# Index scores of two heads on the two halves of the array's rows, and one bank for the probabilities' transposes

## Chip, cores and metric

One core of a Trainium2 chip. The metric is the time of one execution on the device in microseconds; the lower the better. The time before is the median of three runs.

## What is computed

A two-layer decoder step over a prompt of 2048 tokens and a small sample group. The change lies in layer 0, in the sparse attention of the prompt. For each query a lightning indexer scores all earlier keys, the best 256 are kept, and attention runs over those:

```python
N_HEADS, N_KV_HEADS, HEAD_DIM, N_IDX_HEADS, IDX_DIM, TOPK_MAX, SEQ = 8, 2, 128, 16, 64, 256, 2048

def indexer_select(qi, wi, ki, q_pos, k_sel):
    dots = jnp.einsum('thd,ld->thl', qi.astype(F32), ki.astype(F32))
    score = jnp.einsum('th,thl->tl', wi.astype(F32), jax.nn.relu(dots))
    admissible = jnp.arange(ki.shape[0])[None, :] <= q_pos[:, None]
    score = jnp.where(admissible, score, -jnp.inf)
    _, idx = lax.top_k(score, k_sel)
    valid = idx <= q_pos[:, None]
    return idx, valid
```

The dots contract over 64 values only, half of the array's 128 rows. The results are held to the precision of float32, so the kernel splits each float32 operand into a part that the fast format float32r holds exactly (hi) and the rest (lo), and adds up the products of the parts.

## The kernel before

The program has three phases. Phase A projects all tokens (tiles of 128 tokens, groups of 360 to 512 output columns, each product as three matmuls hi x hi, lo x hi and hi x lo by `mm3`, L327). Phase B is the attention over query tiles, in groups of two tiles in the order of `B_ORDER` (L135). Phase C is the recurrent layer. Tiles are allocated from pools with a fixed number of buffers, and a scheduler of the framework sets the order of the instructions on each engine from their dependences, priorities and buffers; each engine then works in that order.

**Index scores** (`indexer`, L1197). Units are pieces of up to 512 keys of a query tile (`widths`, L1126). For the first group, tiles 14 and 15, `index` (L1101) in `phase_a` weaves them into the end of the projection; for the others `phase_b` (L1483) merges them with the attention of the group before. `index_queries` (L1177) loads four heads of a query block (`qiload`), splits hi and lo on POOL into the two halves of 128 columns (`qis`), transposes each head on PE (`qips`), and ACT copies the four to `qiT`: rows 0 to 63 hold the head's hi, rows 64 to 127 its lo. The keys stand in `ki_hi` and `ki_lo`, each twice, in rows 0 to 63 and again in rows 64 to 127 (`prep_index`, L1149). So two matmuls over all 128 rows (L1218, L1219) give one head's dots with all four products of parts, in a PSUM tile `dots` of one bank. ACT applies relu (L1222), and the weighted sum over heads goes on on POOL for the first `gp` heads (3 by `GP_HEADS`, L138; L1225 to L1228) and on DVE for the others (L1230). POOL's heads of a unit are issued a unit ahead, between DVE's heads of the unit before.

**Attention** (`attend_unit` L1404, `attend_scores` L1424, `attend_values` L1446). For each head PE computes the scores `s` in pieces of up to 512 keys, DVE adds the mask and takes the maximum, ACT takes the exponential (`sp`, L1442). For the head before, PE transposes the probabilities in fours into `pt_ps` (L1465), ACT copies them to `pt` (L1467), and PE multiplies with the values into `o_ps` (L1455; one fp32 matmul of the program is two in the trace). The queries' transposes `qps` (L1416) and two small ones use the same PSUM tag.

**PSUM.** There are eight banks. In phase B two are for `s`, three for `dots` (which `qips`, `kps` of `prep_keys` and, at the end, the tiles of `first_chunk` use too), two for `pt_ps` and `qps`, one for `o_ps`. While the index is woven into phase A, four banks are for `dots`.

Of the kernel before, what the change touches and what calls it, by code (L numbers as in the profile page):

```python
# [11 lines left out]
F32 = mybir.dt.float32  # L12
F32R = mybir.dt.float32r
# [4 lines left out]
ALU = mybir.AluOpType  # L18
# [119 lines left out]
GP_HEADS = (3, 3, 3, 3, 3, 3, 3)  # L138
# [848 lines left out]
def phase_a(k):  # L987
    nc, tc = k.nc, k.tc
    with ExitStack() as es:
# [111 lines left out]
        def index():  # L1101
# [3 lines left out]
            with (  # L1105
                tc.tile_pool(name="a_ps3", reuse_waits="tile", bufs=4, space=PSUM) as pd,
# [70 lines left out]
def index_queries(k, qt, hh, pool, pd, tag):  # L1177

    nc = k.nc
    qi = pool.tile([P, 4, ID], F32, tag="qiload", name="qiload", bufs=1)  # L1180
    nc.sync.dma_start(qi, k.qi_d[qt][:, hh * 256 : hh * 256 + 256].rearrange("p (h d) -> p h d", d=ID))
    qs = pool.tile([P, 4, 2 * ID], F32R, tag="qis", name="qis", bufs=1)
    nc.gpsimd.tensor_scalar(qs[:, :, :ID], qi, 1.0, 0.0, ALU.mult, ALU.add)
    nc.gpsimd.tensor_tensor(qs[:, :, ID:], qi, qs[:, :, :ID].bitcast(F32), ALU.subtract)
    t = pool.tile([P, 4, P], F32R, tag="qiT", name="qiT", bufs=5)
    ps = pd.tile([P, 4, P], F32, tag=tag, name="qips", bufs=PS_BUFS.get(tag))
    for j in range(4):
        nc.tensor.transpose(ps[:, j, :].bitcast(F32R), qs[:, j, :], k.ident_r)
    nc.scalar.copy(t, ps)
    return t  # L1190
# [6 lines left out]
def indexer(k, tiles, gp, scores, pool, gpool, spool, stag, pd, dtag, ttag, pq=None):  # L1197
# [12 lines left out]
    def head(u, h):  # L1210
        qt, c, w = units[u]
        if qt not in sc:
            sc[qt] = spool.tile([P, S], F32, tag=stag, name="score", bufs=2)
            scores.append(sc[qt])
        acc = sc[qt][:, c : c + w]
        q = qT[qt, h // 4][:, h % 4, :]
        ps = pd.tile([P, 512], F32, tag=dtag, name="dots", bufs=PS_BUFS.get(dtag))
        nc.tensor.matmul(ps[:, :w], q, k.ki_hi[:, c : c + w], start=True, stop=False)  # L1218
        nc.tensor.matmul(ps[:, :w], q, k.ki_lo[:, c : c + w], start=False, stop=True)  # L1219
        eng, rp, tag, bufs = (nc.gpsimd, gpool, *(("relu", 3) if gpool is pool else ("relu_g", 2))) if h < gp else (nc.vector, pool, "relu", 3)  # L1220
        r = rp.tile([P, 512], F32, tag=tag, name="relu", bufs=bufs)
        nc.scalar.activation(r[:, :w], ps[:, :w], AF.Relu, bias=0.0, scale=1.0)  # L1222
        sg = k.sg_all[:, qt, h : h + 1]
        if h == 0:
            eng.tensor_scalar(acc, r[:, :w], sg, 0.0, ALU.mult, ALU.add)  # L1225
        elif h < gp:
            eng.tensor_scalar(r[:, :w], r[:, :w], sg, 0.0, ALU.mult, ALU.add)
            eng.tensor_tensor(acc, acc, r[:, :w], ALU.add)  # L1228
        else:
            eng.scalar_tensor_tensor(acc, r[:, :w], sg, acc, ALU.mult, ALU.add)  # L1230

    load(5 - len(qT))
    for h in range(gp):
        head(0, h)
    every = (IH - gp) // max(gp, 1)
    for u, (qt, c, w) in enumerate(units):
        for n, h in enumerate(range(gp, IH)):
            head(u, h)
            if gp and n % every == 0 and n // every < gp and u + 1 < len(units):
                head(u + 1, n // every)  # L1240
            if h % 4 == 3:
                if c + w == (qt + 1) * P:
                    del qT[qt, h // 4]
                    load(1)
                yield w
        if c + w == (qt + 1) * P:
# [236 lines left out]
def phase_b(k):  # L1483
    nc, tc = k.nc, k.tc
    with ExitStack() as es:
# [5 lines left out]
        pd = es.enter_context(tc.tile_pool(name="b_pd", reuse_waits="tile", bufs=3, space=PSUM))  # L1491
        pps = es.enter_context(tc.tile_pool(name="b_pt", reuse_waits="tile", bufs=2, space=PSUM))
# [630 lines left out]
```

## Time and profile before

| | us |
|---|---|
| median of three runs (3116.81 to 3122.61) | 3120.4 |
| the profiled execution | 3123.55 |
| its span, first to last instruction | 3121.8 |

| engine | busy us | share |
|---|---|---|
| PE (matmuls) | 2892.9 | 93% |
| PEld (weight loads) | 2398.5 | 77% |
| DVE | 2119.0 | 68% |
| ACT | 1656.3 | 53% |
| POOL | 1239.1 | 40% |

Matmuls are pipelined: the duration of one is its latency, several overlap, and what one takes of PE is the distance from its start to the start of the next. A load of weights belongs to each matmul and has a record of its own under PEld. The index scores run from 1037 to 1965 us, the attention from about 1235 to 2170 us.

### The profile page before, as it was taken

Reading aid. Unit: us, or ns where it says so; the run is one execution under the profiler, and the core shown is the slowest. Engines: PE = TensorE matmul, PEld = TensorE weight load, DVE = VectorE, ACT = ScalarE, POOL = GpSimd, SP = SyncE. Lnnn points to the kernel's source line nnn. Section 1 sums busy time; section 2 is a strip of 40 time slices with the busy share of each in tenths; the row PEclk is TensorE's granted clock in tenths of the full one; section 3 lists DMA queues with packets and bytes.
Section 4 is the critical chain, followed back from the end, with each engine's and each line's share of the span. In section 5 each row is a group of like instructions: output and inputs, shape, how many; then the busy total and the mean of one; then the engine's idle time right before and its main releaser. Section 6 shows DMA issues by size and latency. Waiting matters only on the chain. (4 is left out here: it accounts for less than half of the span.)

```text
span 3121.8 us, 46940 instructions
## 1 busy us (share of the span) xinstructions
PE 2892.9 (93%) x16289; PEld 2398.5 (77%) x16289; DVE 2119.0 (68%) x4600; ACT 1656.3 (53%) x3087; POOL 1239.1 (40%) x1277
## 2 busy tenths in 40 slices
PE   6999998889899998899999999998989989999998
PEld 2999885677567887688878888888767777777766
DVE  6755578944444876886788788634786486485486
ACT  5533322543333566777877776644664454464463
POOL 2634445405552442422332332024434544544643
PEclk8999998998989999899999999999999999999989
DMA  7654421245554212200100111133224524423422
GB/s 243 193 155 153 149 73 46 67 136 153 174 164 136 72 58 92 68 16 27 38 30 27 34 37 36 60 122 131 86 68 149 157 71 136 159 85 110 147 75 91
DMA packets 202014, 314.13 MB, mean 101 GB/s; under 512 B 25651, under 2 KB 119487, under 8 KB 201758
## 3 DMA queue, kind: packets, MB, share of 16 engines
q1 hardware_dynamic: 151482, 213.72, 21.5%
q0 software_dynamic: 15792, 51.92, 5.4%
q10 hardware_dynamic: 34484, 45.34, 4.5%
q8 instruction: 129, 2.11, 0.3%
q14 instruction: 127, 1.04, 0.1%
HBM read 254.56 MB, written 56.34 MB: 100 GB/s over the span
## 5 line engine op out<-in xcount | busy, mean ns | idle before, releaser
L1651 POOL TENSOR_TENSOR wlo<-wraw,whi 128x512 fp32r<-128x512 f32 x288 | 415.2, 1457 | 503.4 <-ACT whi L1650 433.9
L1230 DVE SCALAR_TENSOR_TENSOR score<-relu,sg_all,score 128x512 f32<-128x512 f32 (+2 forms) x494 | 363.1, 737 | 82.4 <-ACT relu L1222 64.5
L331 PE MATMUL zps<-whi,hhi 128*128 128x512 f32 (+2 forms) x1024 | 394.9, 387 | 19.7 <-ACT z_q L365 12.0
L333 PE MATMUL zps<-whi,hlo 128*128 128x512 f32 (+2 forms) x1024 | 391.5, 383 | 4.7 <-issue 4.6
L332 PE MATMUL zps<-wlo,hhi 128*128 128x512 f32 (+2 forms) x1024 | 392.7, 384 | 3.3 <-issue 3.2
L1222 ACT ACTIVATE relu<-dots 128x512 f32<-128x512 f32 (+2 forms) x608 | 314.4, 550 | 135.6 <-PE dots L1219 73.8
L1455 PE MATMUL o_ps<-v,pt 128*128 128x128 f32 x2176 | 300.7, 278 | 7.3 <-ACT pt L1467 6.7
L1455 PEld LDWEIGHTS o_ps<-v,pt 128*128 128x128 f32 x2176 | 284.2, 193 | 25.4 <-ACT pt L1467 11.5
L1650 ACT CAST whi<-wraw 128x512 fp32r<-128x512 f32 x288 | 175.5, 617 | 189.8 <-PE ops L333 92.3
L1218 PE MATMUL dots<-ki_hi,qiT 128*128 128x512 f32 (+2 forms) x608 | 249.7, 413 | 14.3 <-ACT relu L1222 10.6
L331 PEld LDWEIGHTS zps<-whi,hhi 128*128 128x128 f32 x1024 | 197.5, 193 | 61.9 <-ACT z_q L365 14.1
L1219 PE MATMUL dots<-ki_lo,qiT 128*128 128x512 f32 (+2 forms) x608 | 227.0, 375 | 0.0
L333 PEld LDWEIGHTS zps<-whi,hlo 128*128 128x128 f32 x1024 | 197.5, 193 | 35.1 <-issue 7.8
L332 PEld LDWEIGHTS zps<-wlo,hhi 128*128 128x128 f32 x1024 | 197.9, 193 | 33.6 <-issue 6.3
L1467 ACT COPY pt<-pt_ps 128x512 f32<-128x512 f32 (+3 forms) x320 | 163.5, 526 | 84.6 <-PE pt_ps L1465 79.4
L332 PE MATMUL zps<-hlo,whi 128*128 128x512 f32 x512 | 201.9, 394 | 0.0
L331 PE MATMUL zps<-hhi,whi 128*128 128x512 f32 x512 | 198.6, 395 | 3.2 <-ACT hhi L180 2.0
L333 PE MATMUL zps<-hhi,wlo 128*128 128x512 f32 x512 | 200.1, 393 | 0.0
L189 POOL TENSOR_TENSOR rs<-ms,mhalf 128x1 f32<-128x1 f32 (+4 forms) x85 | 80.0, 943 | 279.3 <-DVE ms L188 267.1
L1442 ACT ACTIVATE sp<-sp,neg 128x128 f32<-128x128 f32 (+15 forms) x128 | 154.3, 1206 | 65.9 <-POOL neg L1441 64.1
L1465 PE MATMUL pt_ps<-const,sp 128*128 128x128 f32 x1088 | 173.8, 275 | 3.5 <-ACT sp L1442 2.9
L555 ACT COPY s_kT<-s_tp 128x512 f32<-128x512 f32 x128 | 75.1, 586 | 166.6 <-PE s_dots L564 135.5
(582 smaller groups left out, 7325.7 us busy)
## 6 DMA issues: line engine op xcount, KB each, us to landing
wraw<-in_lru_w_in SPq DMA_DIRECT2D x128, 256.0 KB
wraw<-in_attn_w_out SPq DMA_DIRECT2D x64, 256.0 KB
wraw<-in_lru_w_out SPq DMA_DIRECT2D x64, 256.0 KB
wraw<-in_attn_w_in SPq DMA_DIRECT2D x28, 512.0 KB
wraw<-in_attn_w_in ACTq DMA_DIRECT2D x20, 512.0 KB
ada_raw<-in_ada_w SPq DMA_DIRECT2D x16, 512.0 KB
qi_d<-z_qi SPq DMA_DIRECT2D x32, 256.0 KB
q_d<-z_q SPq DMA_DIRECT2D x32, 256.0 KB
```

Source lines behind the costliest of these rows:

```text
L331: mm(ps, ah, bh, start=start, stop=False)
L332: mm(ps, ah, bl, start=False, stop=False)
L333: mm(ps, al, bh, start=False, stop=stop)
L1218: nc.tensor.matmul(ps[:, :w], q, k.ki_hi[:, c : c + w], start=True, stop=False)
L1219: nc.tensor.matmul(ps[:, :w], q, k.ki_lo[:, c : c + w], start=False, stop=True)
L1222: nc.scalar.activation(r[:, :w], ps[:, :w], AF.Relu, bias=0.0, scale=1.0)
L1230: eng.scalar_tensor_tensor(acc, r[:, :w], sg, acc, ALU.mult, ALU.add)
L1455: nc.tensor.matmul(u.o[:, j, :], pt[:, i, :], k.v_sb[k0 + i][:, u.kv * HD : (u.kv + 1) * HD], start=(k0 + i == 0), stop=(k0 + i == u.qt),)
L1465: nc.tensor.transpose(pt_ps[:, i, :], sp[:, (k0 + i) * P : (k0 + i + 1) * P], k.ident)
L1467: nc.scalar.copy(pt[:, :n, :], pt_ps[:, :n, :])
L1650: nc.scalar.copy(hi, raw)
L1651: nc.gpsimd.tensor_tensor(lo, raw, hi.bitcast(F32), ALU.subtract)
```

## The change

Two heads are computed together. `index_queries` no longer splits before the transpose: it transposes two heads at once (one in the first 64 columns, the other in the last 64), and splits afterwards, ACT copying the hi part and DVE subtracting for the lo part. In `qiT` rows 0 to 63 now belong to the even head and rows 64 to 127 to the odd one, and hi and lo are different columns. `pair` issues three products for each head (hi x hi, hi x lo of the keys, lo x hi; the product of the two lo parts is left out), each over 64 rows, the two heads in turns, into a PSUM tile of two banks, one for each head. The program gives these matmuls the array's rows 0 to 63 and 64 to 127. Relu is one instruction over both heads for DVE's heads (and for POOL's in phase A). POOL takes 4 heads instead of 3. In phase B `dots` becomes two tiles of two banks, and `pt_ps` and `qps` share one bank instead of two; `first_chunk` takes one tile of two banks for its four products.

```diff
-GP_HEADS = (3, 3, 3, 3, 3, 3, 3)
+GP_HEADS = (4, 4, 4, 4, 4, 4, 4)
...
-                tc.tile_pool(name="a_ps3", reuse_waits="tile", bufs=4, space=PSUM) as pd,
+                tc.tile_pool(name="a_ps3", reuse_waits="tile", bufs=2, space=PSUM) as pd,
...
-    qi = pool.tile([P, 4, ID], F32, tag="qiload", name="qiload", bufs=1)
-    nc.sync.dma_start(qi, k.qi_d[qt][:, hh * 256 : hh * 256 + 256].rearrange("p (h d) -> p h d", d=ID))
-    qs = pool.tile([P, 4, 2 * ID], F32R, tag="qis", name="qis", bufs=1)
-    nc.gpsimd.tensor_scalar(qs[:, :, :ID], qi, 1.0, 0.0, ALU.mult, ALU.add)
-    nc.gpsimd.tensor_tensor(qs[:, :, ID:], qi, qs[:, :, :ID].bitcast(F32), ALU.subtract)
-    t = pool.tile([P, 4, P], F32R, tag="qiT", name="qiT", bufs=5)
-    ps = pd.tile([P, 4, P], F32, tag=tag, name="qips", bufs=PS_BUFS.get(tag))
-    for j in range(4):
-        nc.tensor.transpose(ps[:, j, :].bitcast(F32R), qs[:, j, :], k.ident_r)
-    nc.scalar.copy(t, ps)
+    qi = pool.tile([P, 2, 2 * ID], F32, tag="qiload", name="qiload", bufs=2)
+    nc.sync.dma_start(qi, k.qi_d[qt][:, hh * 256 : hh * 256 + 256].rearrange("p (h d) -> p h d", d=2 * ID))
+    t = pool.tile([P, 2, 2, P], F32R, tag="qiT", name="qiT", bufs=5)
+    ps = pd.tile([P, 2, P], F32, tag=tag, name="qips", bufs=PS_BUFS.get(tag))
+    for j in range(2):
+        nc.tensor.transpose(ps[:, j, :], qi[:, j, :], k.ident)
+    split_ps(k, t[:, 0], t[:, 1], ps)
     return t
...
-        q = qT[qt, h // 4][:, h % 4, :]
-        ps = pd.tile([P, 512], F32, tag=dtag, name="dots", bufs=PS_BUFS.get(dtag))
-        nc.tensor.matmul(ps[:, :w], q, k.ki_hi[:, c : c + w], start=True, stop=False)
-        nc.tensor.matmul(ps[:, :w], q, k.ki_lo[:, c : c + w], start=False, stop=True)
...
+        q = qT[qt, h // 4]
+        j = h % 4 // 2
+
+        ps = pd.tile([P, 2, 512], F32, tag=dtag, name="dots", bufs=PS_BUFS.get(dtag))
+        kc = slice(c, c + w)
+        for a, b, n in ((0, k.ki_hi, 0), (0, k.ki_lo, 1), (1, k.ki_hi, 2)):
+            for r in range(2):
+                rows = slice(r * ID, r * ID + ID)
+                nc.tensor.matmul(ps[:, r, :w], q[rows, a, j, :], b[rows, kc], start=(n == 0), stop=(n == 2))
+        eng = nc.gpsimd if h < gp else nc.vector
+        if h < gp and gpool is not pool:
+            rr = [gpool.tile([P, 512], F32, tag="relu_g", name="relu", bufs=2)[:, :w] for _ in range(2)]
+            for n in range(2):
+                nc.scalar.activation(rr[n], ps[:, n, :w], AF.Relu, bias=0.0, scale=1.0)
         else:
-            eng.scalar_tensor_tensor(acc, r[:, :w], sg, acc, ALU.mult, ALU.add)
+            both = pool.tile([P, 2, 512], F32, tag="relu", name="relu", bufs=2)
+            nc.scalar.activation(both[:, :, :w], ps[:, :, :w], AF.Relu, bias=0.0, scale=1.0)
+            rr = [both[:, n, :w] for n in range(2)]
...
-        pd = es.enter_context(tc.tile_pool(name="b_pd", reuse_waits="tile", bufs=3, space=PSUM))
-        pps = es.enter_context(tc.tile_pool(name="b_pt", reuse_waits="tile", bufs=2, space=PSUM))
+        pd = es.enter_context(tc.tile_pool(name="b_pd", reuse_waits="tile", bufs=2, space=PSUM))
+        pps = es.enter_context(tc.tile_pool(name="b_pt", reuse_waits="tile", bufs=1, space=PSUM))
...
-            ps = [pps.tile([P, 2, 256], F32, tag=tag, name="ops") for _ in range(2)]
+            ps4 = pps.tile([P, 4, 256], F32, tag=tag, name="ops")
+            ps = [ps4[:, 0:2], ps4[:, 2:4]]
```

The scheduler makes another order of the same work. On PE, in the attention, before (dots are the index scores, s the attention's, pt_ps the transposes of the probabilities):

```order
L1465 MATMUL pt_ps<-const,sp 128x128 x4
L1218 MATMUL dots<-ki_hi,qiT 128x256
L1219 MATMUL dots<-ki_lo,qiT 128x256
L331 MATMUL s<-kT_hi,qTh 128x384
L332 MATMUL s<-kT_lo,qTh 128x384
L333 MATMUL s<-kT_hi,qTl 128x384
L1218 MATMUL dots<-ki_hi,qiT 128x256
L1219 MATMUL dots<-ki_lo,qiT 128x256
```

and after, in the same stage (an "x2" of dots is the couple on the two halves of the rows):

```order
L1222 MATMUL dots<-ki_hi,qiT 128x256 x2
L1222 MATMUL dots<-ki_lo,qiT 128x256 x2
L1222 MATMUL dots<-ki_hi,qiT 128x256 x2
L331 MATMUL s<-kT_hi,qTh 128x512
L332 MATMUL s<-kT_lo,qTh 128x512
L331 MATMUL s<-kT_hi,qTh 128x384
L332 MATMUL s<-kT_lo,qTh 128x384
L1222 MATMUL dots<-ki_hi,qiT 128x512 x2
L1222 MATMUL dots<-ki_lo,qiT 128x512 x2
L1222 MATMUL dots<-ki_hi,qiT 128x512 x2
L1483 MATMUL pt_ps<-const,sp 128x128 x4
```

Single heads, as two matmuls, have become pairs of six matmuls, which still stand between matmuls over the whole array.

The transposes of the probabilities, on PE, before, with the tiles' numbers; the two tiles are two banks:

```order
L333 MATMUL s_18863<-kT_hi_13726,qTl_18623 128x512
L1465 MATMUL pt_ps_18839<-const_60,sp_18736 128x128 x4
L1465 MATMUL pt_ps_18852<-const_60,sp_18736 128x128 x4
L1218 MATMUL dots_18195<-ki_hi_10814,qiT_17530 128x512
L1219 MATMUL dots_18195<-ki_lo_10815,qiT_17530 128x512
```

and after; the two tiles are the same bank, one after the other:

```order
L1473 MATMUL o_ps_23759<-v8_13610,pt_23792 128x128
L1483 MATMUL pt_ps_23839<-const_60,sp_23758 128x128 x4
L1483 MATMUL pt_ps_23852<-const_60,sp_23758 128x128 x4
L1473 MATMUL o_ps_23759<-v0_13602,pt_23844 128x128
L1473 MATMUL o_ps_23759<-v1_13603,pt_23844 128x128
```

The second four stand right behind the first in both, and in the new order the copy by ACT of the first four lies between them.

## Rows read from the trace of the kernel before

**Rows 1.** The page: span, and busy us (share) xinstructions of each engine.
```profile
span 3121.8 us, 46940 instructions
PE 2892.9 (93%) x16289; PEld 2398.5 (77%) x16289; DVE 2119.0 (68%) x4600; ACT 1656.3 (53%) x3087; POOL 1239.1 (40%) x1277
```

**Rows 2.** Table of stretches: length, busy us (instructions) by engine, PE's clock, DMA share, GB/s.
```profile
1030.00:1130.00 100.00, 100.00 (x472) 83.24 (x472) 85.81 (x161) 59.09 (x108) 54.05 (x54) 1.00 0.22 71
...
1340.00:2130.00 790.00, 756.25 (x5309) 686.85 (x5309) 584.48 (x1778) 550.97 (x1070) 221.27 (x326) 0.99 0.14 45
```

**Rows 3.** List by shape, 1030 to 2180 us: busy us, mean ns, idle before, releasers.
```profile
L1218 PE MATMUL dots<-ki_hi,qiT 128*128 128x512 f32 x400 | 175.8, 440 | 11.6 <-ACT relu L1222 8.0 <-DVE tk_up L1294 2.2 <-DVE tk_dn L1295 0.9
...
L1218 PE MATMUL dots<-ki_hi,qiT 128*128 128x384 f32 x112 | 44.3, 396 | 2.4 <-ACT relu L1222 2.4
...
L1218 PE MATMUL dots<-ki_hi,qiT 128*128 128x256 f32 x96 | 30.0, 322 | 0.2 <-ACT relu L1222 0.2
```

**Rows 4.** Timeline of PE at three places: start us, us, line, operation.
```profile
1187.36 0.39 PE L1219 MATMUL dots<-ki_lo,qiT 128*128 128x512 f32 x1
1187.59 0.39 PE L1218 MATMUL dots<-ki_hi,qiT 128*128 128x512 f32 x1
...
96.17 0.34 PE L332 MATMUL zps<-wlo,hhi 128*128 128x384 f32 x1
96.34 0.34 PE L333 MATMUL zps<-whi,hlo 128*128 128x384 f32 x1
...
1504.24 0.29 PE L1218 MATMUL dots<-ki_hi,qiT 128*128 128x256 f32 x1
1504.37 0.28 PE L1219 MATMUL dots<-ki_lo,qiT 128*128 128x256 f32 x1
```

**Rows 5.** Timeline of PE: 32 matmuls in turns on four quarters of the columns.
```profile
784.21 1.08 PE L933 MATMUL sa_o<-sa_v,sa_pT 128*32 128x128 f32 x32
```

**Rows 6.** Timeline of PE: six fp32 matmuls in a line, in the attention.
```profile
1763.73 0.83 PE L1455 MATMUL o_ps<-v,pt 128*128 128x128 f32 x6
```

**Rows 7.** Timeline of PE at 503 us: two matmuls of 4 rows among full ones.
```profile
503.24 0.40 PE L331 MATMUL zps<-whi,hhi 128*128 128x512 f32 x1
503.47 0.39 PE L332 MATMUL zps<-wlo,hhi 128*128 128x512 f32 x1
503.79 0.48 PE L723 MATMUL ss_nps<-ss_mnew,ones 4*128 4x128 f32 x2
504.20 0.50 PE L333 MATMUL zps<-whi,hlo 128*128 128x512 f32 x1
504.54 0.40 PE L331 MATMUL zps<-whi,hhi 128*128 128x512 f32 x1
```

**Rows 8.** Timeline of the weight loads (PEld) at the same place.
```profile
503.24 0.19 PEld L332 LDWEIGHTS zps<-wlo,hhi 128*128 128x128 f32 x1
503.79 0.29 PEld L723 LDWEIGHTS ss_nps<-ss_mnew,ones 4*128 4x128 f32 x2 [0.36 <-issue]
504.20 0.19 PEld L333 LDWEIGHTS zps<-whi,hlo 128*128 128x128 f32 x1
```

**Rows 9.** Timeline of PE: three transposes right behind matmuls on quarters of the columns.
```profile
785.65 0.55 PE L886 MATMUL sa_ktp<-const,sa_k 128*128 128x128 f32 x3
```

**Rows 10.** Timeline of PE: the query transposes of one block of four heads.
```profile
1505.31 0.46 PE L1188 MATMUL qips<-ident_r,qis 128*128 128x128 f32 x4
```

**Rows 11.** List by shape, as rows 3: ACT's copy of four transposes.
```profile
L1467 ACT COPY pt<-pt_ps 128x512 f32<-128x512 f32 x224 | 129.0, 590 | 63.7 <-PE pt_ps L1465 62.1 <-PE o_ps L1455 0.7
```

**Rows 12.** Waits, 1285 to 2130 us: who waited for whom, us, times, longest us.
```profile
PEld dots L1218 <- ACT relu L1222: 16.1, 21, 2.8
...
PE pt_ps L1465 <- ACT pt L1467: 0.5, 2, 0.3
```

**Rows 13.** List by shape, as rows 3: ACT's relu.
```profile
L1222 ACT ACTIVATE relu<-dots 128x512 f32<-128x512 f32 x400 | 229.5, 603 | 100.1 <-PE dots L1219 56.5 <-DVE score L1230 24.8 <-DMA v<-out_v_prompt 3.8
...
L1222 ACT ACTIVATE relu<-dots 128x256 f32<-128x256 f32 x96 | 35.1, 390 | 10.6 <-PE dots L1219 4.7 <-DVE score L1230 1.4 <-PE pt_ps L1465 1.2
```

More of the change, by code (lines that the diff above doesn't have):

```diff
@@ L1208, in load, with pair @@
         del k.index_todo[:n]
-    def head(u, h):
+    def pair(u, h):
         qt, c, w = units[u]
@@ L1215, in head @@
         acc = sc[qt][:, c : c + w]
-        q = qT[qt, h // 4][:, h % 4, :]
-        ps = pd.tile([P, 512], F32, tag=dtag, name="dots", bufs=PS_BUFS.get(dtag))
-        nc.tensor.matmul(ps[:, :w], q, k.ki_hi[:, c : c + w], start=True, stop=False)
-        nc.tensor.matmul(ps[:, :w], q, k.ki_lo[:, c : c + w], start=False, stop=True)
-        eng, rp, tag, bufs = (nc.gpsimd, gpool, *(("relu", 3) if gpool is pool else ("relu_g", 2))) if h < gp else (nc.vector, pool, "relu", 3)
-        r = rp.tile([P, 512], F32, tag=tag, name="relu", bufs=bufs)
@@ L1222, in head @@
[L1222 to L1228, printed above, removed]
-        else:
-            eng.scalar_tensor_tensor(acc, r[:, :w], sg, acc, ALU.mult, ALU.add)
+        q = qT[qt, h // 4]
@@ new lines, in pair, with done @@
+        for n in range(2):
+            sg = k.sg_all[:, qt, h + n : h + n + 1]
+            r = rr[n]
+            if h + n == 0:
+                eng.tensor_scalar(acc, r, sg, 0.0, ALU.mult, ALU.add)
+            elif h < gp:
+                eng.tensor_scalar(r, r, sg, 0.0, ALU.mult, ALU.add)
+                eng.tensor_tensor(acc, acc, r, ALU.add)
+            else:
+                eng.scalar_tensor_tensor(acc, r, sg, acc, ALU.mult, ALU.add)
+    def done(qt, hh):
+        del qT[qt, hh]
+        load(1)
@@ L1232, in indexer @@
     load(5 - len(qT))
-    for h in range(gp):
-        head(0, h)
-    every = (IH - gp) // max(gp, 1)
+    for h in range(0, gp, 2):
+        pair(0, h)
+    pairs = range(gp, IH, 2)
+    every = len(pairs) // (gp // 2)
     for u, (qt, c, w) in enumerate(units):
[L1237 to L1246, printed above, removed]
+        last = c + w == (qt + 1) * P
+        if last:
+            for hh in range(gp // 4):
+                done(qt, hh)
+        for n, h in enumerate(pairs):
+            pair(u, h)
+            if n % every == 0 and n // every < gp // 2 and u + 1 < len(units):
+                pair(u + 1, n // every * 2)
+            if last and h % 4 == 2:
+                done(qt, h // 4)
+            yield 8 * w / (IH - gp)
+        if last:
```

## The prediction

> **What bounds the kernel now.** I read the page first: PE is busy 93% of the span, no other engine over 68% [rows 1]. The change touches only the index scores and what shares PSUM with them, so I then read the table of stretches for the time in which they run, about 1037 to 2130 us. There PE is the engine that is nearly always busy, 100 of 100 us while the scores are woven into the projection and 756 of 790 us in the attention, at a granted clock of 1.00 and 0.99, which is the 2.4 GHz level; DVE and ACT follow with 74% and 70% [rows 2]. So a microsecond that PE gains or loses there is nearly a microsecond of the kernel, about 5% of it falling on time in which PE waits anyway.
>
> The list by shape gives the number of products: 400 of the first kind (and as many of the second) are 512 wide, 112 are 384 wide, 96 are 256 wide [rows 3]. Two heads make a pair: 200, 56 and 48 pairs, 304 in all. The durations in that list (440 ns) are latencies and overlap; what a matmul takes of PE is the distance to the next start in the timeline: 0.23 us at 512 columns, 0.17 to 0.18 at 384, 0.12 to 0.13 at 256 [rows 4].
>
> **The products.** Before, a pair takes four matmuls of 128 rows. After, it takes six of 64 rows, in three couples, one on each half of the array. If the two of a couple run side by side, a pair takes three matmul times, one fewer: 200 x 0.23 + 56 x 0.174 + 48 x 0.125 = 46.0 + 9.7 + 6.0 = **61.7 us less** on PE. The trace has no couple on halves of the rows, but it has matmuls on four quarters of the columns: 32 matmuls of 128 columns finish in 1.08 us [rows 5]. A plain matmul of that shape has 0.11 us ((0.83 - 0.28) / 5 [rows 6]), so 32 in a line would take 3.5. Parts of the array do run side by side, and I take it that halves of the rows do too.
>
> **The way in and out.** A matmul on part of the array between two on all of it is what the change brings most of. The nearest rows are two matmuls of 4 rows and 128 weight columns in a stream of projection matmuls [rows 7]: the start before them lies 0.32 us ahead instead of 0.23; they end, and the second full matmul after them starts at 504.54. From 503.47 that is 1.07 us, for work that has 0.23 + 2 x 0.11 + 0.23 = 0.68 without a change of shape. So one excursion costs 0.39 us, call it 0.38 with the stream's pace of 0.235. The weight loads show half of it: in the stream a load starts a whole matmul ahead of its own, while across the change the load starts with its matmul, at 503.79 and 504.20 [rows 8], so that the first matmul on either side waits for its weights too.
>
> The Trainium skill ("TensorEngine Tiling (Array Packing)", Key Properties) says that a change of tiling mode, unlike a change of tile, drains the engine. The trace agrees, and prices it: 0.09 us a change, besides the load. By that page's table of theoretical speedups alone, which puts a contraction of 64 rows at up to twice the rate and has no price for a change, the kernel would come out 61.7 us faster.
>
> What decides is the number of excursions. In the changed order on PE the 304 pairs stand in 249 unbroken rows of dots: the scheduler puts them between transposes, score products and projections, 181 of them as single pairs and 56 as two. 130 are followed by products (s, zps, o_ps), 119 by transposes. After a change the first transpose is held less than a product: three of them take 0.55 us where 0.27 + 2 x 0.11 = 0.49 is usual [rows 9], 0.06 in place of 0.10. So 130 x 0.38 + 119 x 0.33 = 49.4 + 39.3 = **88.7 us more**. The bounds: 249 x 2 x 0.09 = 44.8 if the weight loads hide as they do in a stream, and 88.7 + 249 x 0.10 = 113.6 if the loads of the two halves come one after the other. I take 88.7, from the nearest row with as many weight columns. Even a single pair at 512 columns loses: 0.23 saved, 0.33 to 0.38 paid.
>
> **The query transposes.** 224 become 112, without POOL's two operations ahead of each block. Four take 0.46 us [rows 10], (0.46 - 0.25) / 3 = 0.07 each, so 15.7 us; the new ones are plain fp32 like those at 0.11 us, 12.3 us: **3.4 less**. The halves are now split after the transpose on ACT and DVE; DVE gains that and gives up one head in sixteen to POOL, POOL gains the head and loses the two operations. POOL is busy 40% and works a unit ahead; I cost both at nothing, and if DVE's subtraction is late it holds one of only two tiles for dots.
>
> **One bank for the probabilities.** The transposes of the next four blocks can't start before ACT has copied the last four. The bank turns round in about 0.27 + 0.59 us: the transpose's latency, the copy [rows 11]. In the changed order 30 of 353 places have less PE work than that between two uses: 8 have none at all (8 x 0.85 = 6.8), 8 have two score products (0.46 us, 8 x 0.39 = 3.1), 8 have three (0.53 to 0.75, 2.5), the others 1.6; together **14 us more**. Below, nothing: with two banks PE waited 0.5 us for a copy in all [rows 12], and a wait may fall where PE would have waited anyway. Above, 60: ACT works in order, and a copy behind an exponential of 1 to 2 us comes late. I take 14, since ACT gets lighter.
>
> **ACT's relu.** One instruction over two heads saves the fixed part: 603 ns at 512 columns and 390 at 256 [rows 13] make 176 ns fixed, x 244 fewer instructions = 43 us of ACT. What PE waits for relu is 16.1 us [rows 12]; a shorter relu over twice the columns can give back some and the two large tiles in place of three small ones can take some, so I take 0, with 16 either way. The sample's output projection, whose four products now free their banks together, is four places and stays at 0.
>
> **The sum**: -61.7 + 88.7 - 3.4 + 14 = 37.6, less 5% of the 88.7 that fall on idle PE time, 4.4: +33.2 us. The profiled execution took 3123.55 us (span 3121.8), 3.1 over the median of the runs shown, 3120.4. So I forecast 3156.8 on the profiled execution's terms and **3154 us** against the median, 1.1% slower.
>
> **The rivals.**
> 1. *Faster, because the weight loads hide.* If PE loads the other half's weights while the first half works, and the full array's while the halves drain, only the drain is left: -61.7 + 44.8 - 3.4 = -20 us, the bank's waits covered by a lighter ACT: 3100 us, down to 3085 where relu's waits shrink too. It decides by one number: below 0.26 us an excursion ((61.7 + 3.4) / 249), 0.21 with the bank's 14, the change gains. For it: on one mode a load does start a matmul ahead. Against it: in rows 8 none does across a change. Chance 0.24. The Trainium skill ("TensorE: Matmul & The Clock Gate", Part 3, The mechanism) says that loads for row groups that don't conflict are pulled ahead of matmuls in flight; it would do just this, and rows 8 show no such load over a change of mode.
> 2. *No change.* The excursion costs about 0.26 because part of them follow a wait of PE, and the rest cancels: 3120 us. For it: 5% idle is an average, and dots often follow a wait. Chance 0.08.
> 3. *The bank rules.* Copies stand behind exponentials, PE's order can't give way, and 14 becomes 60: 3200 us. For it, 59 of the 320 copies now stand right behind an exponential on ACT, 42 before; against it, those 0.5 us. Chance 0.10.
> 4. *The halves run one after the other*: the change doesn't do what it says. Three matmul times more than forecast for each pair, 3 x 61.7 = 185 us over the forecast, 3340 us. Rows 5 speak against it, though on columns. Chance 0.05.
>
> The forecast itself has 0.53, and within it 3130 to 3178. From 3095 to 3195 the range takes in the forecast, no change, most of rival 1 and half of rival 3; out are rival 4, the upper half of 3 and the lower end of 1, under 0.2 together. Within 0.2%, 6 us, is about what a measurement of this kernel can tell from no change; faster by more has rival 1 and a rest of the forecast and of no change, 0.26; the same 0.11; slower 0.63.
>
> **What would show it.** Right or wrong, step by step: in the timeline of PE two dots matmuls should start within some 10 ns of each other and couples 0.23 us apart (side by side); the start after the matmul ahead of a row of dots should come about 0.1 us late and the first couple should last 0.1 longer (way in), and so on the way out; the weight load of the first dots of a row should start with its matmul. PE's wait of pt_ps for pt should go from 0.5 to some 10 to 20 us. The attention should end later, relative to the projection, by most of the 33 us, and what follows it should not change. I would be wrong if the way in and out took under 0.2 us together, or if the second start of a couple came 0.2 us after the first.

## The result, and the profile after

| | before | after |
|---|---|---|
| median of four runs each, us | 3118.6 | 3279.7 |
| lowest and highest | 3109.8 to 3122.6 | 3273.6 to 3284.7 |
| ratio, 95% interval | 1 | 1.0521 [1.0497, 1.0545] |

The change costs about 161 us, 5.2%; 3154 had been forecast, 1.1% slower, and the range ended at 3195. The page of after, engine by engine, against [rows 1]:

```profile
span 3283.0 us, 47238 instructions
PE 2959.2 (90%) x16785; PEld 2352.6 (72%) x16785; DVE 2140.5 (65%) x4618; ACT 1632.8 (50%) x2843; POOL 1237.8 (38%) x1241
```

No engine has become the bound: all shares fall, PE's from 93% to 90%. Most of the lost time is time in which they wait for each other. Where it lies is seen from one operation that both kernels have 1088 times, the transposes of the probabilities (view of one tile: line, engine, operation, durations, first and last start). Before:

```profile
L1465 PE MATMUL pt_ps<-const,sp x1088: 270/273/476, 1235.4 to 2162.9; 128*128 128x128 f32 x182
```

and after:

```profile
L1483 PE MATMUL pt_ps<-const,sp x1088: 270/273/478, 1242.0 to 2329.4; 128*128 128x128 f32 x182
```

From the first to the last of them, which I call **the attention's stretch** from here on, it was 927.5 us and is 1087.4: all but a few us of the loss is in there. What lies behind the attention has its old length (953 and 951 us from the last o_ps to the end). The table of stretches of after, beside [rows 2]:

```profile
1135.00:1215.00 80.00, 80.00 (x474) 61.59 (x474) 47.46 (x62) 42.26 (x54) 22.66 (x22) 1.00 0.12 41
1340.00:2130.00 790.00, 696.55 (x4771) 552.67 (x4769) 558.24 (x1675) 496.87 (x809) 203.54 (x263) 0.96 0.08 26
```

In the projection PE stays busy all the time. In the attention it was busy for 756 of 790 us and is for 697, DVE loses 26 us and ACT 54, and the granted clock falls from 0.99 to 0.96, a mix of the 2.4 GHz level and more of 1.2. The waits from 1285 to 2130 us: those of PE and PEld stand beside [rows 12], which lack two rows of before,

```profile
ACT pt L1467 <- PE pt_ps L1465: 66.7, 85, 2.3
...
PE dots L1218 <- ACT relu L1222: 6.4, 10, 2.6
```

and these are those of after:

```profile
ACT pt L1485 <- PE pt_ps L1483: 108.1, 103, 3.7
...
PEld dots L1222 <- ACT relu L1230: 42.8, 39, 3.3
...
PEld pt_ps L1483 <- ACT pt L1485: 37.9, 43, 3.7
...
PE dots L1222 <- ACT relu L1230: 30.4, 27, 2.8
...
PE pt_ps L1483 <- ACT pt L1485: 23.1, 29, 3.3
```

PE's wait for the copy went from 0.5 to 23.1 us (10 to 20 forecast), PEld's wait of dots for relu from 16.1 to 42.8, PE's own from 6.4 to 30.4, and ACT in its turn waits 108 us for transposes in place of 67. Both engines work in order; each stands where the other is late. Over the whole stretch PE idles 146 us where it idled 49.

The couples themselves behave as forecast. PE's timeline of after in the projection, one excursion with two pairs in it, beside [rows 7]:

```profile
1100.00 0.40 PE L331 MATMUL zps<-whi,hhi 128*128 128x512 f32 x1
1100.23 0.39 PE L332 MATMUL zps<-wlo,hhi 128*128 128x512 f32 x1
1100.56 0.51 PE L1222 MATMUL dots<-ki_hi,qiT 64*128 64x512 f32 x2
1100.90 0.40 PE L1222 MATMUL dots<-ki_lo,qiT 64*128 64x512 f32 x2
1101.14 0.57 PE L1222 MATMUL dots<-ki_hi,qiT 64*128 64x512 f32 x4
1101.55 0.34 PE L1222 MATMUL dots<-ki_lo,qiT 64*128 64x384 f32 x2
1101.73 0.34 PE L1222 MATMUL dots<-ki_hi,qiT 64*128 64x384 f32 x2
1102.00 0.50 PE L333 MATMUL zps<-whi,hlo 128*128 128x512 f32 x1
1102.33 0.40 PE L331 MATMUL zps<-whi,hhi 128*128 128x512 f32 x1
```

A row with x2 is a couple, started some 3 ns apart (median of the trace); couples follow 0.24 us apart, and from one pair to the next nothing is lost. The way in: 1100.23 to .56 is 0.33 in place of 0.235, the first couple lasts 0.34 in place of 0.235; the way out: 1101.73 to 1102.00 is 0.27 in place of 0.175, and the matmul after it 0.33. Together 0.39 us, the sum that rows 7 gave. PE's weight loads there, beside [rows 8]:

```profile
1100.00 0.19 PEld L332 LDWEIGHTS zps<-wlo,hhi 128*128 128x128 f32 x1
1100.55 0.19 PEld L1222 LDWEIGHTS dots<-ki_hi,qiT 64*128 64x128 f32 x2 [0.36 <-ACT relu L1230]
1100.66 0.19 PEld L1222 LDWEIGHTS dots<-ki_lo,qiT 64*128 64x128 f32 x2
...
1101.99 0.19 PEld L333 LDWEIGHTS zps<-whi,hlo 128*128 128x128 f32 x1 [0.26 <-issue]
1102.10 0.19 PEld L331 LDWEIGHTS zps<-whi,hhi 128*128 128x128 f32 x1
```

On either side of the excursion the load starts with its own matmul (1100.55, 1101.99); inside it the next couple's load starts 0.24 ahead. At 1100.55 a wait for relu ended too, so this row alone can't tell which held the load. Counted over the trace, none of the 206 rows of dots that PE enters without idling has its first load more than 0.06 us ahead, and 145 of these have no release near it; of the 230 ways out none has either, where in the kernel before 97% of 421 had.

So the slots (the matmul times that couples save) and the price of an excursion stand, and still the time is 125 us over the forecast. In the expectations ScalarE is ACT, VectorE DVE and GpSimd POOL. The theories for the experiments: **A**, the single bank for the transposes (forecast at 14 us) costs most of it; **B**, the halves cost more than their excursions; **C**, the two large dots tiles or the relu over two heads (forecast at 0); **D**, the fourth head on GpSimd (forecast at 0).

### The profile page after: what moved, and what is told of

Read it like the earlier page. It is cut to its first block, busy times and chain, and to the rows that moved or that the text cites. A ratio compares the mean times of both kernels' runs of the same rounds, so it can differ in the third digit from the quotient of the medians.

```text
span 3283.0 us, 47238 instructions
## 1 busy us (share of the span) xinstructions
PE 2959.2 (90%) x16785; PEld 2352.6 (72%) x16785; DVE 2140.5 (65%) x4618; ACT 1632.8 (50%) x2843; POOL 1237.8 (38%) x1241
## 5 line engine op out<-in xcount | busy, mean ns | idle before, releaser
L1241 DVE SCALAR_TENSOR_TENSOR score<-relu,sg_all,score 128x512 f32<-128x512 f32 (+2 forms) x456 | 344.6, 758 | 85.5 <-ACT relu L1230 70.9
L1473 PE MATMUL o_ps<-v,pt 128*128 128x128 f32 x2176 | 310.5, 286 | 10.9 <-ACT pt L1485 5.6
L1222 PE MATMUL dots<-ki_hi,qiT 64*128 64x512 f32 (+2 forms) x1216 | 258.1, 433 | 68.1 <-ACT relu L1230 34.6
L1230 ACT ACTIVATE relu<-dots 128x1024 f32<-128x1024 f32 (+2 forms) x244 | 223.6, 924 | 166.9 <-PE dots L1222 53.2
L1459 POOL TENSOR_SCALAR neg<-mx 128x1 f32<-128x1 f32 x128 | 37.1, 290 | 502.9 <-DVE mx L1454 423.6
L1222 PEld LDWEIGHTS dots<-ki_hi,qiT 64*128 64x128 f32 x1216 | 122.2, 197 | 145.6 <-ACT relu L1230 52.0
L1483 PE MATMUL pt_ps<-const,sp 128*128 128x128 f32 x1088 | 187.8, 290 | 35.5 <-ACT pt L1485 27.1
```

The costliest lines, as they stand in the source:

```text
L1222: nc.tensor.matmul(ps[:, r, :w], q[rows, a, j, :], b[rows, kc], start=(n == 0), stop=(n == 2))
L1230: nc.scalar.activation(both[:, :, :w], ps[:, :, :w], AF.Relu, bias=0.0, scale=1.0)
L1241: eng.scalar_tensor_tensor(acc, r, sg, acc, ALU.mult, ALU.add)
L1473: nc.tensor.matmul(u.o[:, j, :], pt[:, i, :], k.v_sb[k0 + i][:, u.kv * HD : (u.kv + 1) * HD], start=(k0 + i == 0), stop=(k0 + i == u.qt),)
L1483: nc.tensor.transpose(pt_ps[:, i, :], sp[:, (k0 + i) * P : (k0 + i + 1) * P], k.ident)
```

## The experiments

Each kernel was timed beside the kernel before on the same chip. That one takes 3079 to 3121 us depending on the chip, so ratios are compared, and us worked out from them at 31 us a point (1%). "Stretch" is the attention's stretch as above, from one trace each. Three chips were used: one for D, A, all but the halves, and the halves with two banks; one for four dots tiles, pairs in tiles of two banks, the changed kernel again and the pairs on full rows; one for the rest. Differences between chips rest on the ratios alone. Every edit also gives the scheduler another order; what of a step is the order and what the buffers was not separated.

| kernel | ratio to before [95%] | stretch, us |
|---|---|---|
| before | 1 | 927.5 |
| D: four heads on GpSimd | 1.0006 [0.9995, 1.0017] | 919.1 |
| A: one bank for the transposes | 1.0210 [1.0193, 1.0227] | 993.7 |
| the same, four dots tiles | 1.0246 [1.0228, 1.0264] | 1011.5 |
| the same, in pairs, GpSimd four | 1.0315 [1.0297, 1.0333] | 1014.6 |
| the same, pairs in tiles of two banks | 1.0393 [1.0364, 1.0422] | 1059.3 |
| the same, relu over both heads: all but the halves | 1.0374 [1.0356, 1.0391] | 1048.5 |
| the changed kernel, again | 1.0532 [1.0502, 1.0563] | 1086.0 |
| two banks kept: pairs on full rows | 1.0030 [1.0010, 1.0050] | 934.8 |
| two banks kept: halves | 1.0456 [1.0437, 1.0474] | 1048.0 |
| A with twice the turns | 1.0746 [1.0726, 1.0766] | 1166.8 |
| changed kernel with twice the turns | 1.1083 [1.1058, 1.1108] | 1263.6 |

**The single bank alone.**

```diff
-        pps = es.enter_context(tc.tile_pool(name="b_pt", reuse_waits="tile", bufs=2, space=PSUM))
+        pps = es.enter_context(tc.tile_pool(name="b_pt", reuse_waits="tile", bufs=1, space=PSUM))
```

> The kernel before with one bank in place of two for the probabilities' transposes, and nothing else of the change. Theory A (the single bank is what the change lost most by: each next group of transposes waits for ScalarE's 0.59 us copy, which waits in order behind the relus): +60 to +110 us. Theory B (the halves of the rows lose it, directly by the excursions and by the half-rate clock around them): +14 us, as the prediction had it, at most +30. Theory C (two large dots tiles and the relu over two heads lose it): +14 us, at most +30. Theory D (VectorE's work given to GpSimd, four heads in place of three): +14 us.

Measured: 2.10% over before, 65 us. Theory A's number, at its lower end; all others had 14. The waits in it from 1180 to 2330 us:

```profile
ACT pt L1467 <- PE pt_ps L1465: 119.3, 113, 5.3
```

and, in the view of PE's waits from 1280 to 2330 us:

```profile
PE pt_ps L1465 <- ACT pt L1467: 27.4, 40, 2.3
PE dots L1218 <- ACT relu L1222: 23.6, 19, 3.3
...
PEld pt_ps L1465 <- ACT pt L1467: 44.2, 55, 2.8
PEld dots L1218 <- ACT relu L1222: 32.9, 37, 3.5
```

The direct wait, 27 us on PE, is under half of the cost. The dots, whose own tiles are untouched, wait 23.6 us for relu where it was 6.4 over the same times before, and ACT's wait for transposes, 119.3 us, was 79.4:

```profile
ACT pt L1467 <- PE pt_ps L1465: 79.4, 94, 5.2
```

A copy that stands on ACT waiting for late transposes holds up the relus behind it. In all PE idles 94 us of the stretch, 49 before. One place where a late copy holds up PE:

```profile
1478.33 0.50 PE L1455 MATMUL o_ps<-v,pt 128*128 128x128 f32 x3
1478.43 1.72 ACT L1292 ACTIVATE mask<-score,tk_cur 128x1664 bf16<-128x1664 f32 x1
...
1479.82 0.40 PE L1219 MATMUL dots<-ki_lo,qiT 128*128 128x512 f32 x1
...
1480.10 1.82 ACT L1292 ACTIVATE mask<-score,tk_cur 128x1792 bf16<-128x1792 f32 x1
...
1481.87 0.62 ACT L1467 COPY pt<-pt_ps 128x512 f32<-128x512 f32 x1
...
1482.54 0.66 PE L1465 MATMUL pt_ps<-const,sp 128*128 128x128 f32 x4 [2.33 <-ACT pt L1467]
```

The copy stands behind two passes of the selection (1.72 and 1.82 us); PE has 1.6 us of dots to do and then idles 2.33 us, since the only bank is full. Worked out from all 320 copies of this trace, a copy starts 0.63 us after the end of the last of its transposes on average, and some 1.85 or more in one of ten; what ACT did last before a late one is relu (97 of 188 us), an exponential (48) or a selection pass (29). In the kernel before the average is 0.79 us, and still 0.61 if a copy behind another group's copy is counted from that one's end: the copies were late there too, and the second bank hid it.

**Full rows, everything else of the change.**

```diff
-        for a, b, n in ((0, k.ki_hi, 0), (0, k.ki_lo, 1), (1, k.ki_hi, 2)):
-            for r in range(2):
-                rows = slice(r * ID, r * ID + ID)
-                nc.tensor.matmul(ps[:, r, :w], q[rows, a, j, :], b[rows, kc], start=(n == 0), stop=(n == 2))
+        for r in range(2):
+            nc.tensor.matmul(ps[:, r, :w], q[:, h % 4 + r, :], k.ki_hi[:, kc], start=True, stop=False)
+            nc.tensor.matmul(ps[:, r, :w], q[:, h % 4 + r, :], k.ki_lo[:, kc], start=False, stop=True)
```

(against the changed kernel, and index_queries as before the change)

> The changed kernel with full-row products again: queries as hi over lo on 128 rows, four products of 128 rows for a pair, four transposes for four heads; the pair's tile of two banks, two of these tiles, the relu over two heads, the one bank for the probabilities' transposes and GpSimd's four heads stay. Against before: theory A +70 to +120 us; theory B +10 to +30 us; theory C +80 to +130 us; theory D +80 to +130 us. The difference from the changed kernel (+161 us) is what the halves cost net: +30 us by the prediction's own terms (-62 of slots, +89 of excursions, +3 of query transposes), over +100 us by theory B.

Measured: 3.74% over before, 116 us. So 7/10 of the loss is there without any half; theory B falls as the main cause, and A, C and D all fit this number. PE's granted clock points the same way (table of stretches, over the whole attention of this kernel):

```profile
1187.00:2237.00 1050.00, 920.95 (x6048) 810.18 (x6048) 719.02 (x2096) 645.49 (x1106) 349.66 (x464) 0.95 0.14 43
```

It is 0.95 here, 0.94 over the attention of the changed kernel and 0.97 before: 102, 139 and 54 us at the 1.2 GHz level. Over half of what came on is there without the halves.

**The changed kernel again**, unedited, on the second chip; full rows ran on the first.

> The changed kernel as it is, so that it stands on the same chip as the experiments beside it. By the ratio of its first runs, 5.2% over before, some +160 us. What it stands over the kernel with full rows and everything else of the change (3.7% over before) is the net of the halves: by the prediction's terms with the excursion at 0.39 us as measured, -62 - 3 + 249 x 0.39 = +32 us; by a theory that the halves also slow what stands around them (half-rate clock after drains, later copies), +50 us or more.

Measured: 5.32%, over the full rows by 1.6 points, with both intervals 1.2 to 1.9, so 49 us, 11 either way, by ratios of two chips. By excursions at 0.39 it would be 32; the other theory's 50 or more fits. In the projection, where PE hardly waits, the halves can be read alone: from the first dots to the last zps the changed kernel takes 187.9 us, full rows 176.2. Of these 12 us, 55 rows of dots make 55 x 0.39 = 21, less 14 for slots, and nearly three pairs more in that stretch some 2.5; 2 us are left over. The other 38 us fall in the attention's stretch.

**The halves without the single bank.** Three dots tiles of one bank, two banks for the transposes, a relu for each head:

```diff
-        ps = pd.tile([P, 2, 512], F32, tag=dtag, name="dots", bufs=PS_BUFS.get(dtag))
+        ps = [pd.tile([P, 512], F32, tag=dtag, name="dots", bufs=PS_BUFS.get(dtag)) for _ in range(2)]
...
-                nc.tensor.matmul(ps[:, r, :w], q[rows, a, j, :], b[rows, kc], start=(n == 0), stop=(n == 2))
+                nc.tensor.matmul(ps[r][:, :w], q[rows, a, j, :], b[rows, kc], start=(n == 0), stop=(n == 2))
...
-        pd = es.enter_context(tc.tile_pool(name="b_pd", reuse_waits="tile", bufs=2, space=PSUM))
-        pps = es.enter_context(tc.tile_pool(name="b_pt", reuse_waits="tile", bufs=1, space=PSUM))
+        pd = es.enter_context(tc.tile_pool(name="b_pd", reuse_waits="tile", bufs=3, space=PSUM))
+        pps = es.enter_context(tc.tile_pool(name="b_pt", reuse_waits="tile", bufs=2, space=PSUM))
```

> The changed kernel with the halves kept, but three dots tiles of one bank (a pair takes two), a relu for each head, and two banks for the probabilities' transposes, as before. Theory A: +20 to +50 us against before, the rest of the +161 being gone. Theory B: +120 to +160 us. Theory C: +40 to +70 us, since a pair takes two of three tiles and the next has to wait for one. Theory D: +100 us or more.

Measured: 4.56%, 141 us: theory B's number, and D's, but in a kernel whose couples have come apart. PE's timeline of this kernel:

```profile
1500.51 0.39 PE L1222 MATMUL dots<-ki_hi,qiT 64*128 64x256 f32 x2
...
1501.07 1.16 PE L1474 MATMUL o_ps<-v,pt 128*128 128x128 f32 x8
1502.16 0.49 PE L1222 MATMUL dots<-ki_hi,qiT 64*128 64x512 f32 x1
1502.49 0.39 PE L1222 MATMUL dots<-ki_lo,qiT 64*128 64x512 f32 x1
1502.72 0.39 PE L1222 MATMUL dots<-ki_hi,qiT 64*128 64x512 f32 x1
1503.05 0.38 PE L1474 MATMUL o_ps<-v,pt 128*128 128x128 f32 x1
```

At 1502.16 one head goes alone: with two tiles of three in use only one is free, and the scheduler takes the couple apart. 922 of the 1824 products have no partner within 60 ns, so the slots are 902 / 2 + 922 = 1373 against 1216 on full rows, more instead of fewer, and PE goes in and out 402 times instead of 249. So this run prices more excursions than the change has.

**Its counterpart on full rows**, against that kernel (`index_queries` is as before the change too):

```diff
-        for a, b, n in ((0, k.ki_hi, 0), (0, k.ki_lo, 1), (1, k.ki_hi, 2)):
+        for b, n in ((k.ki_hi, 0), (k.ki_lo, 1)):
             for r in range(2):
-                rows = slice(r * ID, r * ID + ID)
-                nc.tensor.matmul(ps[r][:, :w], q[rows, a, j, :], b[rows, kc], start=(n == 0), stop=(n == 2))
+                nc.tensor.matmul(ps[r][:, :w], q[:, h % 4 + r, :], b[:, kc], start=(n == 0), stop=(n == 1))
```

> Full-row products, but in the pair's order (both heads in turns) on two of three dots tiles of one bank, a relu for each head, two banks for the probabilities' transposes, four heads on GpSimd: the counterpart on full rows of the kernel that had the halves without the single bank (+142 us against before). Theory B (the halves cost by excursions, 402 of them there): that kernel less 402 x 0.39 - 62 - 3 = 92 us, so +50 us. Theory F (a pair that takes two of three tiles can't be worked ahead, and that is what costs): +110 to +140 us.

Measured: 0.30%, 9 us. Theory F falls, and B's +50 is missed as well, since the halves cost more than the 92 us that it took off. With two banks kept neither the order by pairs nor GpSimd's fourth head costs much. The halves cost 4.26 points, 132 us, here. Counted, 157 slots more at 0.203 us (61.7 / 304) and 402 excursions at 0.39 make 32 + 157 - 3 = 186; a part falls on time in which PE would have waited: its idle time in the stretch is 54 us on full rows and 28 with the halves.

**Four heads on GpSimd alone.**

```diff
-GP_HEADS = (3, 3, 3, 3, 3, 3, 3)
+GP_HEADS = (4, 4, 4, 4, 4, 4, 4)
...
+        if c + w == (qt + 1) * P:
+            del qT[qt, 0]
+            load(1)
...
-                yield w
+                yield 4 * w / 3
```

(the lines below the first fit the loop to twelve heads left to DVE)

> The kernel before with four heads of a unit on GpSimd in place of three, and nothing else of the change. Theories A, B and C: -10 to +10 us. Theory D: +60 us or more, GpSimd's products ending last before the selection.

Measured: no difference, the interval being -0.05% to 0.17%. Theory D is out, and the zero of the prediction stands.

**The single bank with the freed bank given to the dots** (b_pd 4, b_pt 1):

> The kernel before with one bank for the probabilities' transposes, and the bank that this frees given to the dots: four tiles of one bank, a head each. It has the changed kernel's split of the banks without its pairs. Theory A (the single bank's own turnaround costs): as with the single bank and three tiles, +55 to +65 us. Theory E (the single bank costs since ScalarE falls behind and PE then stands at the dots' tiles; a deeper row of tiles takes it up): +20 to +40 us.

Measured: 2.46%, 76 us. A deeper row of dots tiles takes up nothing; it is even 0.4 points worse than three tiles, which no run here explains. PE's wait for the copy is again some 30 us. Theory E falls; A is nearer, though the time lies above its range.

**The same in pairs, GpSimd four** (the full-row pairs of 0.30% with b_pd 4 and b_pt 1):

> Full rows in the pair's order, four heads on GpSimd, a relu for each head, one bank for the transposes, and the pair's products into two of four dots tiles of one bank, where the counterpart with two tiles of two banks stood 3.9% over before. Theory C2 (the tile of two banks, free only when both heads are evicted, is what costs): as with four tiles and heads one by one, 2.5% over before, +75 us. Theory P (the order by pairs costs, whatever the tiles): 3.7 to 4% over before, +115 to +125 us.

Measured: 3.15%, between the two theories. The order by pairs costs 0.7 points beside a single bank, and the tile of two banks 0.8 more (3.93%), both just outside each other's intervals and across two chips. The second step also changes the order of the four matmuls of a pair, from turns to head by head.

**A relu for each head, in the tile of two banks:**

```diff
-            nc.scalar.activation(both[:, :, :w], ps[:, :, :w], AF.Relu, bias=0.0, scale=1.0)
             rr = [both[:, n, :w] for n in range(2)]
+            for n in range(2):
+                nc.scalar.activation(rr[n], ps[:, n, :w], AF.Relu, bias=0.0, scale=1.0)
```

(against the full rows with everything else of the change)

> Full rows, the pair's tile of two banks, one bank for the probabilities' transposes, four heads on GpSimd, but a relu for each head in place of one over both. Theory C1 (the relu over two heads, 0.92 us in one piece, holds up the copies behind it on ScalarE): better than the kernel with the relu over two heads, +70 to +95 us against before where that one has +114. Theory C2 (the tile of two banks is what costs, since neither half comes free before both are done): the same +114, or up to 20 us more for ScalarE's extra fixed parts.

Measured: 3.93%, where the relu over both had 3.74%: C2, the intervals overlap, and the one long relu does no harm that can be measured.

**Twice the turns of the bank.** The bank is one tile, used as two halves in turns, two blocks and one copy each:

```diff
-        pt_ps = pps.tile([P, 4, P], F32, tag="t", name="pt_ps")
-        for i in range(n):
-            nc.tensor.transpose(pt_ps[:, i, :], sp[:, (k0 + i) * P : (k0 + i + 1) * P], k.ident)
         pt = pool.tile([P, 4, P], F32, tag="pt", name="pt", bufs=3)
-        nc.scalar.copy(pt[:, :n, :], pt_ps[:, :n, :])
+        for a in range(0, n, 2):
+            m = min(2, n - a)
+            pt_ps = half_bank(k)
+            for i in range(a, a + m):
+                nc.tensor.transpose(pt_ps[:, i - a, :], sp[:, (k0 + i) * P : (k0 + i + 1) * P], k.ident)
+            nc.scalar.copy(pt[:, a : a + m, :], pt_ps[:, :m, :])
...
+def half_bank(k):
+
+    k.turn ^= 1
+    return k.bank[:, k.turn]
```

> The kernel before with one bank for the transposes, but the bank used as two halves of two blocks in turns, each with a copy of its own (256 columns), so that PE can fill one half while ScalarE empties the other; the query transposes go through the same halves. Theory A1 (the single bank costs because there is no second buffer while a copy is late): most of the single bank's +64 us comes back, +5 to +35 us over before, the rest being the fixed part of some 250 more copies, 0.18 us each on ScalarE. Theory A2 (PE's writes and ScalarE's reads hinder each other in one bank, or what counts is the number of banks): +64 us or more.

Measured: 7.46%, 231 us. It was meant to give the second buffer back and does not: in its trace none of the 1088 transposes starts while a copy runs, so the two halves, being one tile, were made to wait for each other, and A1 was not tested. PE's writes and ScalarE's reads never met in the bank, so A2's number came without that part of its mechanism; that the number of banks as such counts is not ruled out. What the kernel did is to raise the suspected cost: 576 turns by probabilities instead of 320, and 64 by queries instead of 32, the next transposes waiting for each copy. The waits from 1180 to 2380 us:

```profile
ACT pt L1476 <- PE pt_ps L1475: 234.1, 311, 7.0
...
PEld pt_ps L1475 <- ACT pt L1476: 117.8, 217, 3.6
...
PE pt_ps L1475 <- ACT pt L1476: 63.5, 80, 3.3
...
PE dots L1218 <- ACT relu L1222: 51.6, 52, 4.0
```

The first three are some twice those of the single bank or more, and the dots' wait for relu grows with them, from 28.1 us on PE in the single bank's trace (1180 to 2340 us), though nothing of the dots was touched. More turns at a late copy cost more, but not in proportion: 3.6 times the loss for 1.8 times the turns. The fixed part of 256 more copies, some 45 us of ACT at 0.176 us each, is in it and was not told apart.

> The changed kernel with the transposes' bank used as two halves in turns, as in the experiment beside it. Theory A1, with terms that add up: the changed kernel's +163 us less what the halves of the bank give back in the other kernel, +100 to +130 us. Theory A2: +160 us or more. Theory G (the waits in the changed kernel replace each other, and the two large dots tiles take over where the bank is relieved): +140 to +165 us.

The same in the changed kernel: 10.83%. The extra turns cost 5.5 points there and 5.4 without the rest of the change (7.46 - 2.10). That is some 336 us over before, which A1 and G did not have and A2 only as a lower end; with the extra turns at the same price in both kernels, the terms add up.

## Why the prediction was wrong in size

In points, the steps from before to after are: the single bank 2.10; four small dots tiles 0.36; the order by pairs with GpSimd's fourth head 0.69; the tile of two banks 0.78; the relu over both -0.19; the halves 1.58: 5.32 in all. By its own steps:

- **One bank for the probabilities, 14 us, 0 to 60: the step that failed.** It measured 65 us, alone, and at or above its upper bound (60 to 70 by the interval). "The bank turns round in about 0.27 + 0.59 us" took the copy to start as soon as the transposes end. They end, and with the single bank the copy starts 0.63 us later on average (0.61 to 0.79 already in the kernel before, by the way of counting), so a turn is some 0.6 us longer than costed, and far longer behind a selection pass. The view was there: the starts of the copies in ACT's timeline. The 0.5 us wait of [rows 12] was no evidence that copies are prompt, only that two banks hid them. And only the direct wait was counted: 10 to 20 us were forecast for PE's wait, 23.1 came, but the whole cost of the bank, alone, is over twice the direct wait.
- **ACT's relu and the two large tiles, 0, 16 either way: failed too.** The 16.1 us behind it are the weight loads' row (PEld); PE's own wait was 6.4, and came to 30.4. The relu itself is at zero, as said. The tile of two banks and the order by pairs, with the four tiles' share, cost 1.83 points, 57 us. With two banks for the transposes the order by pairs costs 9 us (3 to 16) and beside a single one 21 (13 to 29), so part of this may be a price of the same coupling: the fewer buffers between two engines that work in order, the more of each one's lateness reaches the other. That is argued, not shown. Two tiles of two banks beside two banks for the transposes were not tried: with the other tiles as they are PSUM has no room for them.
- **The products, -61.7: right.** 1818 of the 1824 half-row products have a partner within 60 ns, and couples of 512 columns are 0.23 us apart (median).
- **The way in and out, 88.7: right in kind, a little low.** 249 rows of dots, as counted from the order. 162 of them have no wait of PE in them and cost 0.389 us on average: medians 0.40 before a product (0.38 said) and 0.35 before a transpose (0.33 said). 249 x 0.389 = 97.
- **The halves together**, -61.7 + 88.7 - 3.4 - 4.4 = 19 us, came to 49, 11 either way. 8 of the difference are the price above. The 4.4 of idle cover went the wrong way: PE idles 129 us of the stretch with full rows and 146 with the halves (151 in the second trace), and the time at the 1.2 GHz level is 102 and 139 us (123). That what starts late behind an excursion reaches ACT late would fit, and is only argued; the rest of the difference, some 22 us, stays open.
- **DVE and POOL at nothing: right for the fourth head** (the run with four heads on GpSimd). DVE's subtraction was not run alone; PE waits 4.9 us for it in the trace of after, from 1280 to 2330 us.
- **What would show it**: the attention does end later by nearly the whole difference, and what follows it is unchanged, as written.

Of the rivals, the third, the bank rules, was the mechanism of the largest single step: it had a chance of 0.10, 60 us and 3200 us. Its price was right for the bank alone; the time came out 80 higher, by the 51 us of pairs, tiles and relu and the 30 of the halves. It named exponentials as what copies stand behind; relus come first. One such place, ACT and PE in the changed kernel:

```profile
1548.44 1.78 ACT L1310 ACTIVATE mask<-score,tk_cur 128x1792 bf16<-128x1792 f32 x1
1548.60 0.50 PE L1222 MATMUL dots<-ki_hi,qiT 64*128 64x512 f32 x2 [0.54 <-ACT relu L1230]
...
1549.17 0.40 PE L1222 MATMUL dots<-ki_hi,qiT 64*128 64x512 f32 x2
...
1550.22 1.99 ACT L1460 ACTIVATE sp<-sp,neg 128x2048 f32<-128x2048 f32 x1
...
1552.21 0.57 ACT L1485 COPY pt<-pt_ps 128x512 f32<-128x512 f32 x1
...
1552.83 1.12 PE L1483 MATMUL pt_ps<-const,sp 128*128 128x128 f32 x4 [3.26 <-ACT pt L1485]
```

One single pair, and then PE idles 3.26 us behind a selection pass, an exponential and the copy; the four transposes then take 1.12 us, where the four of the place above, behind a shorter wait and at the 2.4 GHz level, took 0.66, and the granted clock is at its lower level for 6.8 us from 1551.8 on.

Rival 1, faster since the weight loads hide, is out: by the counts above no load is ahead of its matmul across a change of shape. Here the Trainium skill ("TensorE: Matmul & The Clock Gate", Part 3, The mechanism), by which loads for row groups that don't conflict are pulled ahead of matmuls in flight, holds inside an excursion (0.24 us ahead) and not at its ends. Rival 4, the halves one after the other, is out for the change, and came true in part where the couples were taken apart.

No version beats the kernel before. With the bank kept at two, full rows in pairs come within 0.3%, and the halves, to stay in couples, want two tiles of two banks, for which PSUM has no room beside it.

## What to carry to other kernels

Before taking a buffer away between two engines that both work in order, measure how late the consumer starts on each use (from the end of the producer's last instruction to the start of the copy), over all uses and not at the median: a short wait with two buffers (0.5 us here) said nothing on what one would cost (65), and the direct wait was under half of that. Splitting products over halves of the rows pays only if many such products stand together: each way in and out cost 0.39 us, and a pair saved 0.23 at most. And what must run side by side needs its buffers as one piece: with single banks the scheduler took 922 of 1824 products out of their couples, with one tile for both heads 6.

## What was not expected of the hardware

- The granted clock is lower where PE idles more, though not in step: over the stretch PE idles 49 us before, 94 with the single bank, 129 with full rows and all else of the change and 146 in the changed kernel, and 54, 60, 102 and 139 us of it are at the 1.2 GHz level. There a product of 512 columns takes 0.43 us from start to start in place of 0.235, so a wait behind which the clock falls costs more than the time waited.
- Going over to the half rows costs nearly the same whatever stands there: the start after the last full matmul 0.09 us late, the first couple 0.10 longer, on the way out 0.09 and, before a product, 0.10 again, before a transpose 0.06. Entered the same way, rows of full-row dots cost 0.01 us. The Trainium skill ("TensorEngine Tiling (Array Packing)", Key Properties) says that a change of tiling mode drains the engine; the trace agrees, with the 0.09 us, and has the exposed weight load beside it, which is as large.
